# The last residual turned inside the first block of rows, its last weight sum moved to VectorE, and the restored chunks of y split one by one

## The chip, the cores and the metric

The kernel runs on one NeuronCore of a Trainium2 chip. The metric is the device time of one execution in microseconds, the lower the better. The engines are TensorE (PE, with its weight loads as PEld), VectorE (DVE), ScalarE (ACT), GpSimd (POOL) and SyncE (SP), which issues most transfers.

## The reference

One inference step of a hybrid decoder layer, for 512 prompt tokens and 8 x 4 sample tokens, width 2048: an input projection, an mLSTM branch, a sliding-window attention branch, a gated merge, an output projection, a residual and a layer norm. The change lies in the last lines of the merge:

```python
y = (jax.nn.sigmoid(g_m) * jnp.einsum('btc,cd->btd', br_m, w_proj_m)
     + jax.nn.sigmoid(g_a) * jnp.einsum('btc,cd->btd', br_a, w_proj_a))
out = jnp.einsum('btc,cd->btd', y, w_out)
return _layernorm(DN_ALPHA * x + out, ln_w, ln_b).astype(x.dtype)
```

## The kernel before

All 544 tokens are worked at once, in tiles of 128 output columns by 544 tokens. Products are made of three fp32r products: an operand is split into a high part (a cast on ScalarE, L221 for weights, L283 for all else) and a low part (a subtraction on VectorE, L222 and L284), and high by high, high by low and low by high are summed in PSUM.

The output projection has 16 tiles of columns (ct). Tiles 0 to 3 are plain products. Tiles 4 to 13 are done in five pairs by `paired`, which computes two tiles with seven half products (steps n = 0 to 6) in place of eight, on sums of quarters of the weights and of y. `prepare` makes the weight sum of a step two steps ahead: with `acc` set, the sums other than that of n = 2 which go into one of their own operands are done by a DMA that adds (L684, issued by POOL), the others by VectorE (L686). `half_product` is the TensorE work (L706 with high weights, L708 with low), `gather` takes the seven results together into the two tiles O1 and O2 (L716 to L735; L735, at n = 6, writes the last quarter of O1, which is the state's `c21` after the change). TensorE runs in the order of the program text (a manual schedule); the other engines are ordered by a scheduler, within what `behind` demands.

A finished tile is spawned as `residual_task`: a later `tick` turns it on TensorE, four transposes for the rows of tokens (L1795) and one for 32 odd tokens (L1801), each into a PSUM tile `sm` of a pool of four banks, and VectorE adds it to the rows z (L1797) and zs (L1802). The 32 odd tokens are copied aside first by ScalarE (L1791).

The last 256 columns, tiles 14 and 15, are done the other way round: `rows_of(t)` takes y as the stationary operand and gives 128 tokens by 256 columns, in 16 chunks k of three matmuls (L1885), into one `sm` bank. Its weights, w3, come as four pieces of 512 KB (two halves of k by two column tiles), loaded by `land_rows` (L211) and split by `split_rows` (L283, L284). `add_rows` adds the block to z (L1867), takes its statistics and moments; `finish` normalises and stores (L1848, L1852, L1854). There are four blocks t = 0 to 3; the sample rows come between.

One quarter of y (y21, the even chunks for the second half of the tokens) has lost its place to other forms by then. `land_y21` loads them again from DRAM in three loads (3, 3 and 2 chunks; before, L1950), into tiles of the pool `raw2`, and `restore_y21` splits them into new y21 tiles in four splits. Blocks 2 and 3 of the rows and `sum_others(1)` (L2022) use them. `beside_output` is a list of such side work by step number, one step for each half product of the five pairs. The tail itself reads

```python
tick()
rows_of(0, {13: rest})
add_rows(0)
finish(0)
```

where `rest` ticks once more, exhausts `restored` and calls `sum_others(1)`; that is, ahead of chunk 13, in the order of TensorE and VectorE.

Of the kernel before, what the change touches and what calls it, by code (L numbers as in the profile page):

```python
# [18 lines left out]
ALU = mybir.AluOpType  # L19
# [61 lines left out]
def _build(tc, nc, i, o, es):  # L81
# [11 lines left out]
    V, A, G, PE = nc.vector, nc.scalar, nc.gpsimd, nc.tensor  # L93
# [60 lines left out]
    state = {}  # L154

    def tick():
        for g in list(live):
            if next(g, StopIteration) is StopIteration:
                live.remove(g)
# [65 lines left out]
    @contextmanager  # L225
    def behind(*what):

        with ExitStack() as st:
            for w in what:
                st.enter_context(tc.issue_after(state[w].ins))  # L230
            yield
# [50 lines left out]
    def hilo(src, hi, lo):  # L282
        state["hi"] = A.copy(hi, src)  # L283
        state["lo"] = V.tensor_tensor(out=lo, in0=src, in1=r32(hi), op=ALU.subtract)  # L284
# [394 lines left out]
    def prepare(w, n):  # L679


        def add(out, a, b):
            if w.get("acc") and out == a and n != 2:
                G.dma_start(out=w[out][:], in_=w[b][:], accum_op=ALU.add)  # L684
            else:
                V.tensor_tensor(out=w[out][:], in0=w[a][:], in1=w[b][:], op=ALU.add)  # L686
        if n == 1:
            w["t1"] = raw2()
            add("t1", "b11", "b12")
        elif n == 2:  # L690
            add("b11", "t1", "b22")
        w["hl", n] = split(w[("b11", "t1", "b11", "b21", "b12", "b22", "b21")[n]])
        if n == (1 if w.get("acc") else 3):
            add("b12", "b12", "b22")
        elif n == (3 if w.get("acc") else 4):
            add("b21", "b21", "b11")
# [13 lines left out]
    def gather(w, n):  # L710

        A0, D0, B0 = (w["bank", b][:, :HT] if ("bank", b) in w else None for b in range(3))
        sc = w["scale"]
        if n == 0:
            w["p1"] = pe_.tile([128, HT], F32, tag="p1", name=nm("p1"))
            A.activation(w["p1"][:], A0, AF.Copy, scale=sc)  # L716
            return
        if n == 1:
            w["O1"], w["O2"] = ev(), ev()
        c11, c21 = (w["O1"][:, c:c + HT] for c in (0, HT))  # L720
        c12, c22 = (w["O2"][:, c:c + HT] for c in (0, HT))
        p1 = w["p1"][:]
        if n == 1:
            A.activation(c11, D0, AF.Copy, scale=sc)  # L724
            G.tensor_tensor(out=c22, in0=p1, in1=c11, op=ALU.subtract)  # L725
        elif n == 2:
            V.scalar_tensor_tensor(c12, B0, sc, p1, op0=ALU.mult, op1=ALU.subtract)  # L727
        elif n == 3:
            A.activation(c11, A0, AF.Copy, scale=sc)
        elif n == 4:  # L730
            V.scalar_tensor_tensor(c22, B0, -sc, c22, op0=ALU.mult, op1=ALU.add)  # L731
        elif n == 5:
            V.scalar_tensor_tensor(c12, D0, sc, c12, op0=ALU.mult, op1=ALU.add)
        else:
            V.scalar_tensor_tensor(c21, B0, sc, p1, op0=ALU.mult, op1=ALU.subtract)  # L735

    AHEAD = 400

    def paired(work, first=iter(()), early=False):

        steps = [(w, n) for w in work for n in range(7)]
        ready = 0
        load_a(work[0])
        with nullcontext() if early else behind("raw"):
            load_b(work[0])
        for at, (w, n) in enumerate(steps):

            if early and at == 0:
                next(first)
            while ready < min(at + 3, len(steps)):  # L750
                with tc.high_priority(offset=AHEAD), (behind("wh", "wl") if at == 0 else nullcontext()):
                    prepare(*steps[ready])
                ready += 1
            p = at // 7 + 1
            if n == 4 and "fetch" in w:
                w["fetch"]()
            if p < len(work):
                if n == 3:
                    load_a(work[p])
                elif n == 4:  # L760
                    load_b(work[p])
            half_product(w, n)
            with tc.high_priority(offset=AHEAD):
                gather(w, n)
            next(first, None)
            if n == 6:
                w["end"](w["O1"], w["O2"])
            tick()
# [537 lines left out]
    last = last_sum(s4)  # L1306
# [285 lines left out]
    def form_tile(p, s):  # L1592
        return p.tile([128, 4, 2, HT], F32R, tag="act", name=nm(s))
# [94 lines left out]
    with tc.manual_schedule(engines={PE.engine}):  # L1688
        y11, y21, yo = [], [], ([], [])
# [188 lines left out]
    def rows_of(t, meanwhile={}):  # L1878
        ps = rows[t] = sm()
        at = (0, 128, 272, 400)[t]  # L1880
        for k in range(KT):
            if k in meanwhile:
                meanwhile[k]()
            for n, (a, p) in enumerate(TERMS):
                PE.matmul(ps[:, 0:G3 * 128], (yh, yl)[a](k, at, 128), w_rows(k, p),  # L1885
                          start=(k == 0 and n == 0), stop=(k == KT - 1 and n == 2))
# [51 lines left out]
    def land_rows(half, g):  # L1938
        pieces.append((half, slice(g * 128, g * 128 + 128), load_half(wo, (16 - G3 + g) * 128, half)))
# [4 lines left out]
            hilo(raw[:], *(w[:, :, cs] for w in w3[half]))  # L1944

    landed = []

    def land_y21(j0, n):
        st = raw2()[:].rearrange("p a b -> p (a b)")[:, 0:n * HT].rearrange("p (j t) -> p j t", t=HT)
        nc.sync.dma_start(st, d_y[2 * j0:2 * (j0 + n):2, :, HT:T].rearrange("k p t -> p k t"))  # L1950
        landed.append((j0, n, st))

    def restore_y21():
        for j0, n, st in landed:
            for j in range(j0, j0 + n):
                if j in (j0, 4):
                    e = min(j0 + n, 4) if j < 4 else j0 + n
                    hilo(st[:, j - j0:e - j0], *(y21[j // 4][:, j % 4:j % 4 + e - j, p] for p in range(2)))
                    yield

    def beside_output():

        s4.extend(form_tile(act3, "s4") for _ in range(2))
        todo = {11: [lambda: load_rows(2)], 18: [lambda: load_rows(3)],
                27: [lambda: land_rows(0, 0)], 30: [open_rows], 31: [split_rows, lambda: land_rows(0, 1)],
                32: [lambda: land_rows(1, 0), lambda: land_rows(1, 1)],
                33: [split_rows, lambda: land_y21(0, 3)],
                34: [split_rows, split_rows, lambda: land_y21(3, 3), lambda: land_y21(6, 2)]}
        for at in range(35):
            for f in todo.get(at, ()):  # L1970
                f()
            yield
# [18 lines left out]
    def projected(p):  # L1991
        ct = 4 + 2 * p

        def end(o1, o2):
            spawn(residual_task(ct, o1, 1))
            spawn(residual_task(ct + 1, o2, 1))
        return dict(wv=wo, cA=ct * 128, cB=ct * 128 + 128, scale=1.0, acc=True, kts=(slice(0, 16, 2), slice(1, 16, 2)), end=end)

    with tc.manual_schedule(engines={PE.engine}):
        paired([projected(p) for p in range(5)], beside_output(), early=True)  # L2000
    y21[:] = [form_tile(actS, "y21") for _ in range(2)]

    def ln_rows(name):
        out = []
# [5 lines left out]

    with behind("raw"):
        lw, lb = ln_rows("ln_w"), ln_rows("ln_b")
    restored = restore_y21()
    ysum = ev(512)[:].rearrange("p (k t) -> p k t", k=KT)
    both_ = ysum.rearrange("p (g j o) (c t) -> p g j o c t", g=2, o=2, c=2)

# [12 lines left out]
    sum_others(0, 2, 3)  # L2029
    with tc.manual_schedule(engines={PE.engine, V.engine}):  # L2030

        def rest():
            tick()
            for _ in restored:
                pass
            sum_others(1)

        tick()
        rows_of(0, {13: rest})
        add_rows(0)  # L2040
        finish(0)
        rows_of(1)
        add_rows(1)
        esY.close()
        d2 = pool(esY, "d2", 1)
        lwq, lbq = (d2.tile([128, 512], F32, name=nm("lnq"))[:] for _ in range(2))
        cq = d2.tile([128, 128], F32, name="cq")
        nc.sync.dma_start(cq[:], i["consts"][:, C_Q:C_Q + 128])
        for q in range(4):
            r, cs = slice(q * 32, q * 32 + 32), slice(q * 512, q * 512 + 512)  # L2050
            nc.sync.dma_start(lwq[r], i["ln_w"][cs].partition_broadcast(32))
            nc.sync.dma_start(lbq[r], i["ln_b"][cs].partition_broadcast(32))
        finish(1)
        parts = sample_rows()
        rows_of(2, {3: lambda: add_sample_rows(parts), 12: lambda: moments(4)})
        finish(4)
        add_rows(2)
        finish(2)
        rows_of(3)
        add_rows(3)  # L2060
        finish(3, (0, 1024, 1664, 2048))
# [31 lines left out]
```

## Time and profile before

| | |
|---|---|
| median of 3 runs | 2477.39 us (2476.89 to 2478.4) |
| the profiled execution | 2476.01 us, of which the span of the profile is 2474.1 |
| PE busy | 2450.5 us, 99% of the span |
| DVE busy | 1832.1 us, 74% |
| ACT busy | 1236.5 us, 50% |
| POOL busy | 389.3 us, 16% |
| last product of the five pairs, first L1885, first L1867 | 2426.36, 2431.78, 2439.23 us from the span's start |

A row of the timeline has the start and the duration in us, the engine, the line, the operation, what is written and read, the count, and in brackets how long the engine had been idle and what ended that. Rows of stretches have the stretch, its length, then for PE, PEld, DVE, ACT and POOL the busy time and the number of instructions, then the granted clock of TensorE (1.00 is full), the busy share of the DMA engines, and GB/s. A row of waits says who waited for whom, for how long in total, how often, and the longest wait.

### The profile page before, as it was taken

What the parts mean: (1) busy time and instruction counts of PE and PEld (TensorE: products, weight loads), DVE (VectorE), ACT (ScalarE), POOL (GpSimd) and SP (SyncE); (2) the same over time, 40 slices, a digit from 0 to 9 for tenths busy, and PEclk for the clock granted to TensorE, in tenths of its full rate; (3) what the DMA queues carried; (4) which work ended last, traced back from release to release, by engine and by line L of the source; (5) the groups of instructions that cost most, each with busy time, mean ns of one, the idle gap of its engine ahead of it and who ended that gap; (6) DMA issues with size and microseconds to landing.
All of it is one profiled execution on the core that took longest, in us unless ns stands there. A gap on an engine that the chain in (4) does not pass through costs nothing. (4 is left out here: it accounts for less than half of the span.)

```text
span 2474.1 us, 48874 instructions
## 1 busy us (share of the span) xinstructions
PE 2450.5 (99%) x19631; PEld 2388.1 (97%) x19631; DVE 1832.1 (74%) x2697; ACT 1236.5 (50%) x2016; POOL 389.3 (16%) x458
## 2 busy tenths in 40 slices
PE   9999999999999999999999999999999999999997
PEld 9999999999999999999999999999999999999996
DVE  5687777777777777788778788887865557777767
ACT  4457766766766775443433444444633324434431
POOL 2121111111111111121111221200000002111211
PEclk9999999999999999999999999999999999999999
DMA  5675666666666545468577575786554549988875
GB/s 162 184 182 139 153 160 157 151 151 160 151 158 159 139 125 152 125 189 264 172 237 250 168 239 173 227 247 180 178 178 162 168 154 285 236 231 232 214 185 162
DMA packets 556803, 453.96 MB, mean 183 GB/s; under 512 B 42833, under 2 KB 465809, under 8 KB 556513
## 3 DMA queue, kind: packets, MB, share of 16 engines
q1 hardware_dynamic: 542448, 399.86, 54.8%
q0 software_dynamic: 14128, 50.99, 11.3%
q8 instruction: 154, 2.52, 0.4%
q14 instruction: 73, 0.59, 0.1%
HBM read 309.37 MB, written 94.22 MB: 163 GB/s over the span
## 5 line engine op out<-in xcount | busy, mean ns | idle before, releaser
L221 ACT CAST wh<-raw 128x1024 fp32r<-128x1024 f32 x640 | 670.3, 1048 | 811.6 <-PE bank L706 649.8
L222 DVE TENSOR_TENSOR wl<-raw,wh 128x1024 fp32r<-128x1024 f32 x640 | 794.8, 1244 | 260.5 <-ACT wh L221 259.2
L686 DVE TENSOR_TENSOR raw<-raw,raw 128x1024 f32<-128x1024 f32 x242 | 309.4, 1278 | 11.5 <-DMA raw<-in_w_in 3.8
L706 PE MATMUL bank<-xk,wh 128*128 128x272 f32 x2272 | 311.6, 289 | 0.0
L706 PEld LDWEIGHTS bank<-xk,wh 128*128 128x128 f32 x2272 | 293.6, 188 | 3.4 <-issue 2.5
L725 POOL TENSOR_TENSOR ev<-p,ev 128x272 f32<-128x272 f32 x84 | 124.7, 1484 | 577.0 <-ACT ev L724 546.9
L708 PE MATMUL bank<-xk,wl 128*128 128x272 f32 x1136 | 164.8, 287 | 0.0
L708 PEld LDWEIGHTS bank<-xk,wl 128*128 128x128 f32 x1136 | 151.4, 188 | 0.0
L684 POOL DMA_DIRECT2D raw<-raw x94 | 81.0, 862 | 446.2 <-DVE raw L686 228.8
L706 PE MATMUL bank<-s4h,wh 128*128 128x272 f32 x568 | 146.8, 291 | 0.0
L706 PE MATMUL bank<-s1h,wh 128*128 128x272 f32 x568 | 146.6, 291 | 0.1
L706 PE MATMUL bank<-n3h,wh 128*128 128x272 f32 x568 | 145.6, 289 | 0.5 <-DVE ev L727 0.5
L706 PE MATMUL bank<-a11h,wh 128*128 128x272 f32 x568 | 145.9, 289 | 0.0
L706 PE MATMUL bank<-n2h,wh 128*128 128x272 f32 x568 | 145.2, 289 | 0.0
L706 PE MATMUL bank<-a11l,wh 128*128 128x272 f32 x568 | 145.1, 288 | 0.0
L706 PE MATMUL bank<-n3l,wh 128*128 128x272 f32 x568 | 144.8, 288 | 0.0
L706 PE MATMUL bank<-s4l,wh 128*128 128x272 f32 x568 | 144.6, 287 | 0.0
L706 PE MATMUL bank<-s1l,wh 128*128 128x272 f32 x568 | 144.6, 287 | 0.0
L706 PE MATMUL bank<-n2l,wh 128*128 128x272 f32 x568 | 144.6, 287 | 0.0
L731 DVE SCALAR_TENSOR_TENSOR ev<-bank,ev 128x272 f32<-128x272 f32 x84 | 37.0, 441 | 125.7 <-PE bank L708 125.6
L246 PE MATMUL bank<-bh,wh 128*128 128x272 f32 x512 | 109.1, 292 | 0.0
L246 PE MATMUL bank<-bh,wl 128*128 128x272 f32 x512 | 108.9, 289 | 0.0
(563 smaller groups left out, 5851.1 us busy)
## 6 DMA issues: line engine op xcount, KB each, us to landing
raw<-in_w_in SPq DMA_DIRECT2D x296, 512.0 KB, 4.9
raw<-raw POOLq DMA_DIRECT2D x94, 512.0 KB, 4.9
C<-in_state_mlstm_C SPq DMA_DIRECT2D x32, 1024.0 KB, 6.5
out<-C SPq DMA_DIRECT2D x64, 512.0 KB, 3.5
raw<-in_w_proj_a SPq DMA_DIRECT2D x32, 512.0 KB, 4.8
raw<-in_w_proj_m SPq DMA_DIRECT2D x32, 512.0 KB, 6.1
raw<-in_w_out SPq DMA_DIRECT2D x32, 512.0 KB, 5.8
d_sga<-ev SPq DMA_DIRECT2D x16, 272.0 KB, 2.0
```

Of the source, the lines that this page charges most:

```text
L221: state["wh"] = A.copy(wh[:], raw[:])
L222: state["wl"] = V.tensor_tensor(out=wl[:], in0=raw[:], in1=r32(wh[:]), op=ALU.subtract)
L246: PE.matmul(ps[ALL, f, 0:w], a[:, kk], b(k, c, w), start=(k == 0 and n == 0), stop=(k == 15 and n == 2))
L684: G.dma_start(out=w[out][:], in_=w[b][:], accum_op=ALU.add)
L686: V.tensor_tensor(out=w[out][:], in0=w[a][:], in1=w[b][:], op=ALU.add)
L706: PE.matmul(ps, wh[:, k], x(p, k), start=(first and k == 0 and p == 0), stop=False, skip_group_check=True)
L708: PE.matmul(ps, wl[:, k], x(0, k), start=False, stop=(k == 7), skip_group_check=True)
L725: G.tensor_tensor(out=c22, in0=p1, in1=c11, op=ALU.subtract)
L731: V.scalar_tensor_tensor(c22, B0, -sc, c22, op0=ALU.mult, op1=ALU.add)
```

## The change

Three things. In `prepare`, the sum of n = 3 of the last pair (marked `last`) is made by VectorE in place of the adding DMA. The first load of y21 stands at step 30 of the side work, its tiles are made at step 33, and the first of the four splits is done there; a split of y21 is held behind `c21` of the pair before. In the tail, the restoring and `sum_others(1)` come ahead of chunk 1 of the first block, and the two ticks that turn the last pair's tiles come ahead of chunk 10, no tick ahead of the block.

```diff
         def add(out, a, b):
-            if w.get("acc") and out == a and n != 2:
+            if w.get("acc") and out == a and n != 2 and not (n == 3 and "last" in w):
                 G.dma_start(out=w[out][:], in_=w[b][:], accum_op=ALU.add)
...
-            V.scalar_tensor_tensor(c21, B0, sc, p1, op0=ALU.mult, op1=ALU.subtract)
+            state["c21"] = V.scalar_tensor_tensor(c21, B0, sc, p1, op0=ALU.mult, op1=ALU.subtract)
...
+    def open_y21():
+        y21[:] = [form_tile(actS, "y21") for _ in range(2)]
...
-                    hilo(st[:, j - j0:e - j0], *(y21[j // 4][:, j % 4:j % 4 + e - j, p] for p in range(2)))
+                    with behind("wh", "wl", "c21"):
+                        hilo(st[:, j - j0:e - j0], *(y21[j // 4][:, j % 4:j % 4 + e - j, p] for p in range(2)))
                     yield
+
+    restored = restore_y21()
...
-                27: [lambda: land_rows(0, 0)], 30: [open_rows], 31: [split_rows, lambda: land_rows(0, 1)],
+                27: [lambda: land_rows(0, 0)], 30: [open_rows, lambda: land_y21(0, 3)],
+                31: [split_rows, lambda: land_rows(0, 1)],
                 32: [lambda: land_rows(1, 0), lambda: land_rows(1, 1)],
-                33: [split_rows, lambda: land_y21(0, 3)],
+                33: [open_y21, split_rows, lambda: next(restored)],
                 34: [split_rows, split_rows, lambda: land_y21(3, 3), lambda: land_y21(6, 2)]}
...
-        paired([projected(p) for p in range(5)], beside_output(), early=True)
-    y21[:] = [form_tile(actS, "y21") for _ in range(2)]
+        paired([projected(p) for p in range(4)] + [projected(4) | {"last": True}], beside_output(), early=True)
...
-        def rest():
-            tick()
+        def restore():
             for _ in restored:
                 pass
             sum_others(1)

-        tick()
-        rows_of(0, {13: rest})
+        def residual():
+            tick()
+            tick()
+
+        rows_of(0, {1: restore, 10: residual})
```

How the order of the instructions changes. First TensorE, from the last product of the pairs on; ev_28807 and ev_28808 are O1 and O2, ox the 32 odd tokens. Before:

```order
-L708 MATMUL bank_28823<-yo_27037,wl_28887 128x272 x4
-L1795 MATMUL sm_28998<-cc,ev_28807 128x128 x4
-L1801 MATMUL sm_29004<-cc,ox_27130 32x128
-L1795 MATMUL sm_29008<-cc,ev_28808 128x128 x4
-L1801 MATMUL sm_29014<-cc,ox_27131 32x128
-L1885 MATMUL sm_29017<-w_3817_28811,y_3585_26880 128x256
```

and after, with the chunks between left out:

```order
+L708 MATMUL bank_28825<-yo_27037,wl_28889 128x272 x4
+L1885 MATMUL sm_28999<-w_3817_28811,y_3585_26880 128x256
...
+L1885 MATMUL sm_28999<-w_3819_28813,yo_27038 128x256
+L1795 MATMUL sm_29039<-cc,ev_28807 128x128 x4
+L1801 MATMUL sm_29045<-cc,ox_27130 32x128
+L1795 MATMUL sm_29049<-cc,ev_28808 128x128 x4
+L1801 MATMUL sm_29055<-cc,ox_27131 32x128
+L1885 MATMUL sm_28999<-w_3819_28813,y_3603_27036 128x256
```

The ten transposes moved behind the tenth chunk; the block's sum sm_28999 now takes its bank ahead of the four turned tiles, and the last of these, sm_29055, takes the bank of the first, sm_29039.

Then VectorE at the same place, from the last quarter of O1 to the first L1867. Before:

```order
-L735 SCALAR_TENSOR_TENSOR ev_28807<-bank_28823,p_3807_28755 128x272
-L1797 SCALAR_TENSOR_TENSOR z_27816<-z_27816,sm_28998 128x4x128
-L1802 SCALAR_TENSOR_TENSOR zs<-zs,sm_29004 32x128
-L1797 SCALAR_TENSOR_TENSOR z_27816<-z_27816,sm_29008 128x4x128
-L1802 SCALAR_TENSOR_TENSOR zs<-zs,sm_29014 32x128
-L284 TENSOR_TENSOR y_3834_28978<-raw_3831_28917,y_3834_28978 128x3x272
-L284 TENSOR_TENSOR y_3834_28978<-raw_3832_28948,y_3834_28978 128x272
-L284 TENSOR_TENSOR y_3835_28979<-raw_3832_28948,y_3835_28979 128x2x272
```

and after:

```order
+L735 SCALAR_TENSOR_TENSOR ev_28807<-bank_28825,p_3807_28755 128x272
+L284 TENSOR_TENSOR y_3832_28917<-raw_3834_28952,y_3832_28917 128x272
+L284 TENSOR_TENSOR y_3833_28918<-raw_3834_28952,y_3833_28918 128x2x272
+L284 TENSOR_TENSOR y_3833_28918<-raw_3835_28954,y_3833_28918 128x2x272
+L2026 TENSOR_TENSOR ev_28990<-y_3832_28917 128x4x16
+L2026 TENSOR_TENSOR ev_28990<-y_3833_28918 128x4x16
+L1797 SCALAR_TENSOR_TENSOR z_27816<-z_27816,sm_29039 128x4x128
+L1802 SCALAR_TENSOR_TENSOR zs<-zs,sm_29045 32x128
```

Three splits of y21 and the two sums (L2022 before, L2026 after) moved ahead of the residual's additions; the first and largest split moved further up, ahead of the splits of the last two pieces of weights.

Last, VectorE at the sum of n = 3 of the last pair (raw_28600 is the weight quarter that is added to raw_3797_28635). After:

```order
+L2030 TENSOR_TENSOR ev_28990<-yo_27037,yo_27038 128x4x16 x2
+L686 TENSOR_TENSOR raw_3797_28635<-raw_3797_28635,raw_28600 128x1024
+L727 SCALAR_TENSOR_TENSOR ev_28808<-bank_28825,p_3807_28755 128x272
+L222 TENSOR_TENSOR wl_28822<-raw_28602,wh_28821 128x1024
 L284 TENSOR_TENSOR w_3818_28812<-raw_28691,w_3817_28811 128x8x128
```

L686 was not there before, and L684 of the same tiles has gone from POOL's queue, where it stood last ahead of the five L1831. SP's loads keep their order, of weights and of y. The second, third and fourth piece of weights are loaded into the three tiles `raw`; before, the second took the place of the one read by the low split of n = 4, the third that of the source of the adding DMA, the fourth that of the first piece. After, the second takes the place of L686's source, the third that of the tile split for n = 4, the fourth again that of the first piece.

More of the change, by code (lines that the diff above doesn't have):

```diff
@@ L2012, in _build @@
         lw, lb = ln_rows("ln_w"), ln_rows("ln_b")
-    restored = restore_y21()
     ysum = ev(512)[:].rearrange("p (k t) -> p k t", k=KT)
```

## The prediction

> **What bounds the kernel now.** I read the page's busy shares, then the chain that ended last, then VectorE's waits behind the chain's first row, and then went backwards through the timeline.
>
> ```profile
> PE 2450.5 (99%) x19631; PEld 2388.1 (97%) x19631; DVE 1832.1 (74%) x2697; ACT 1236.5 (50%) x2016; POOL 389.3 (16%) x458
> ```
> ```profile
> 2442.06 0.49 DVE z L1848
> ...
> 2469.06 0.53 DVEq L2089
> ```
> ```profile
> DVE z L1867 <- PE sm L1885: 3.2, 1, 3.2
> DVE mv L1828 <- PE sm L1827: 0.5, 1, 0.5
> DVE zs L1837 <- POOL mv L1831: 0.4, 1, 0.4
> ```
>
> Over the span TensorE is the bound (99%), but the chain from 2442 on is VectorE's. Behind the first L1867 (the first block of rows is added to the residual) VectorE waits only twice more, 0.5 and 0.4 us, both inside the normalisation of the sample rows, which the change leaves alone. So the end lies a fixed time behind that first L1867, and what moves it moves the end by as much. What stands ahead of it, in the timeline and then in stretches of 2 us (the clock is the third number from the right):
>
> ```profile
> 2427.37 0.38 PE L1795 MATMUL sm<-cc,ev 128*128 128x128 f32 x2
> 2427.85 1.04 ACT L283 CAST w<-raw 128x1024 fp32r<-128x1024 f32 x1 [1.02 <-DMA raw<-in_w_out]
> 2428.93 1.23 DVE L284 TENSOR_TENSOR w<-raw,w 128x1024 fp32r<-128x1024 f32 x1 [1.26 <-ACT w L283]
> 2429.01 1.51 ACT L283 CAST y<-raw 128x272 fp32r<-128x272 f32 x3
> 2430.07 0.43 DVE L735 SCALAR_TENSOR_TENSOR ev<-bank,p 128x272 f32<-128x272 f32 x1
> ...
> 2430.56 0.44 PE L1795 MATMUL sm<-cc,ev 128*128 128x128 f32 x2 [2.81 <-DVE ev L735]
> ...
> 2431.04 0.69 DVE L1797 SCALAR_TENSOR_TENSOR z<-z,sm 128x512 f32<-128x512 f32 x1 [0.53 <-PE sm L1795]
> ...
> 2431.78 1.01 PE L1885 MATMUL sm<-w,y 128*128 128x256 f32 x3
> ...
> 2433.10 2.63 DVE L284 TENSOR_TENSOR y<-raw,y 128x816 fp32r<-128x816 f32 x4
> ...
> 2435.65 0.35 DVE L2022 TENSOR_TENSOR ev<-y 128x64 f32<-128x64 f32 x2
> ...
> 2438.68 0.52 PE L1885 MATMUL sm<-w,yo 128*128 128x256 f32 x3
> ...
> 2439.03 0.51 PE L1885 MATMUL sm<-w,y 128*128 128x256 f32 x3
> ...
> 2439.23 0.42 DVE L1867 SCALAR_TENSOR_TENSOR z<-z,sm 128x256 f32<-128x256 f32 x1 [3.23 <-PE sm L1885]
> ```
> ```profile
> 2444.32 0.52 PE L1885 MATMUL sm<-w,yo 128*128 128x256 f32 x3
> ```
> ```profile
> 2430.00:2432.00 2.00, 1.35 (x9) 0.97 (x10) 1.44 (x4) 0.81 (x3) 0.00 (x0) 0.93 1.04 416
> 2432.00:2434.00 2.00, 2.00 (x10) 2.00 (x11) 1.91 (x4) 0.00 (x0) 0.00 (x0) 0.50 0.49 197
> 2434.00:2436.00 2.00, 2.00 (x15) 2.00 (x14) 2.00 (x6) 0.00 (x0) 0.00 (x0) 0.72 0.13 37
> ```
>
> TensorE comes to the turning of the last pair's first tile at 2427.37, does two transposes, and stands 2.81 us: the tile's last quarter (L735) is queued on VectorE behind the split of the last piece of weights (L284 at 2428.93), which waits for ScalarE's cast (2427.85), which waits for that piece's load. Then the granted clock falls to 0.50. The 16 chunks of the first block take 2431.78 to 2439.03, 7.25 us; at full clock a chunk takes (2444.32 - 2439.03) / 15 = 0.353 us and 16 of them 5.65. From 2427.37 to L1867 it is 11.86 us.
>
> **The change part by part.**
>
> *Rows before the residual.* After: TensorE starts the block's chunks where the transposes stood, at 2427.37. Ten chunks end at 2430.90. What the turning costs there, from the pair before, where nothing waited:
>
> ```profile
> 2408.24 0.60 PE L1795 MATMUL sm<-cc,ev 128*128 128x128 f32 x4
> ...
> 2408.68 0.27 PE L1801 MATMUL sm<-cc,ox 128*32 128x128 f32 x1
> ...
> 2408.79 0.60 PE L1795 MATMUL sm<-cc,ev 128*128 128x128 f32 x4
> ...
> 2409.22 0.27 PE L1801 MATMUL sm<-cc,ox 128*32 128x128 f32 x1
> ```
>
> The second L1801 follows 0.98 us behind the first L1795, at 2431.88. Here it must wait: the block's sum holds one of the four PSUM banks, so this fifth tile takes the bank of the first turned tile and needs VectorE's L1797 to have read it. Four transposes (0.60) end at 2431.50; L1797 starts 0.04 later, as after the transposes of 2430.56, takes 0.69, and TensorE follows 0.05 later, as at 2431.78: 2432.28, a wait of 0.40 that before did not exist. The next chunk is 0.11 behind it (2408.68 to 2408.79), the sixteenth five chunks on (2432.39 + 1.77 = 2434.16), and L1867 0.55 behind the start of the sixteenth (2438.68 to 2439.23): 2434.71 instead of 2439.23, 4.52 us earlier. Of this 2.81 is the idle time, 1.60 the slow clock (7.25 - 5.65), the rest the order. The bounds here: with no wait at the fifth tile 4.9; and a group after a short wait can last 0.1 longer, 4.4.
>
> The term of 1.60 rests on the clock's following the gap. The trace has it once: 4.4 us without a product (2427.37 to 2431.78, with the transposes and the stand), then 0.50 for about 3 us, then 1.00. The Trainium skill ("TensorE: Matmul & The Clock Gate", Part 1) says that the clock is halved after an idle window of about 3.4 us and comes back after a busy one, that the window runs freely, so that the place of the change varies from run to run, and (Part 4) that transposes do not count as busy. By that rule an execution whose window lay otherwise would show no slow chunks before the change, and the sum would be 2.9 instead of 4.5; the trace agrees with the rule, as far as one fall in one execution can. The turning behind chunk 10, 1.5 us without a product, is shorter than the stand that preceded this fall.
>
> *The last sum on VectorE.* One L686 is added there, one L684 leaves POOL's queue.
>
> ```profile
> 2404.03 1.23 DVE L686 TENSOR_TENSOR raw<-raw,raw 128x1024 f32<-128x1024 f32 x1
> ...
> 2415.65 0.89 POOL L684 DMA_DIRECT2D raw<-raw  x1 [1.85 <-DVE wl L222]
> ...
> 2416.08 0.43 DVE L727 SCALAR_TENSOR_TENSOR ev<-bank,p 128x272 f32<-128x272 f32 x1
> ...
> 2418.35 2.16 PE L706 MATMUL bank<-n,wh 128*128 128x272 f32 x16
> ...
> 2420.79 1.05 ACT L221 CAST wh<-raw 128x1024 fp32r<-128x1024 f32 x1 [1.78 <-DMA raw<-raw]
> ...
> 2421.63 0.44 DVE L731 SCALAR_TENSOR_TENSOR ev<-bank,ev 128x272 f32<-128x272 f32 x1 [1.72 <-PE bank L708]
> ```
>
> L686 stands ahead of L727, so L727 and three splits move by 1.23 us. TensorE's L706 at 2418.35 adds onto the bank that L727 reads; L727 now ends at 2416.08 + 1.23 + 0.43 = 2417.74, 0.6 in time. The splits are made up for by L731, ahead of which VectorE idled 1.72. Price nothing; if that cover were gone, 1.23 less the 0.6, that is 0.6 us, on TensorE. POOL has nothing else to do there, so its 0.89 brings nothing; the sum's transfer had held up the cast at 2420.79, and no product waited for that.
>
> *Loads.* SP's order keeps its places; what each load waits for changes.
>
> ```profile
> 2417.67 4.04 SPq L211 DMA_DIRECT2D raw<-in_w_out  x3
> ...
> 2421.80 2.01 SPq L1950 DMA_DIRECT2D raw<-d_y  x2
> ...
> 2422.81 1.05 ACT L283 CAST w<-raw 128x1024 fp32r<-128x1024 f32 x1 [0.97 <-DMA raw<-in_w_out]
> ```
> ```profile
> SPq L211 <- DMA raw<-raw: 3.1, 2, 2.6
> ```
>
> Before, the second of three weight loads waited 2.6 us for the transfer of the sum to let go of its source; that is gone. Now they are free at L686's end (2417.3), at the end of the moved split (2416.43 row's place + 1.2: about 2418.9) and one split later (about 2420), so the last is issued near 2420 instead of 2421.3. Landing took 5.1 us (2417.67 to 2422.81) and for the last one 6.5 (to 2427.85): it lands between 2425.1 and 2426.5. Cast and split (1.04, 1.23) end by 2428.9, and L735, whose product ends at 2427.5, by 2429.3. Chunk 8, the first that needs these weights, comes at 2427.37 + 8 x 0.353 = 2430.19; the tile's last quarter is wanted at 2431.1. Both are hidden behind the chunks, with 1.3 and 1.8 us to spare.
>
> *Restored chunks.* Their first split moves ahead; the other three (1.64 of the 2.63, by elements) and the two L2022 (0.35) now stand between L735 and L1797: 2429.3 + 2.0 = 2431.3, 0.2 ahead of the 2431.54 at which L1797 wants to start. This is the narrowest cover; each us beyond it costs one. The last load of y is issued behind the split of the pair's last weights as before (by 2423.8, the end of that row), and in the trace of before its cast was never late (three casts from 2429.01 without a gap, so it had landed by 2430.0).
>
> Sum: 4.5 us off the profiled execution's 2476.01, 2471.5. That execution lies 1.4 under the median of the runs, 2477.39; taken off the median, 2472.9.
>
> **The rivals.** *The loads land no sooner.* The 1.04 and 1.23 of the last piece then stay at 2427.85 and 2428.93, L735 ends at 2430.5, the three splits and L2022 at 2432.5, and L1797 starts 0.9 late; chunk 8 still finds its weights (2430.16 against 2430.19). Gain 3.6, 2473.8. For it: the last piece took 6.5 us among the loads of y and the norm's weights, which stay. Against: its issue moves by 1.3 us and 512 KB of traffic go.
>
> *The slow clock isn't the gap's.* If runs without the profiler never fell to 0.50 there, or fall after the change too, 1.60 of the 4.5 is lost: gain 2.9, 2474.5. For it: 2.81 us is short, and the row of 2430 shows 0.93 still, so that the fall came about 1.3 us after TensorE had started again. Against: the clock is 1.00 in all neighbouring stretches. The page's freely running window, weighed above, would be its cause.
>
> *Slower.* VectorE takes its queue in order, so the last load of y now stands ahead of L1797, and so of TensorE's fifth tile, and of all that follows. From its landing to L1797 it is 0.5 (cast), 0.7 (split), 0.35. It costs nothing until 2430.0, then one for one; beyond 2.8 us the clock would fall again. The gain is gone when it lands at about 2433, some 9.5 us after its issue. The longest median in the list of transfers around here is 7.7, for the norm's weights, queued behind it:
>
> ```profile
> ln<-in_ln_w SPq DMA_DIRECT2D x2, 512.0 KB, 7.7
> ```
>
> **How the numbers follow.** Forecast (gain 3.9 to 4.9) 0.62; loads no sooner (3.2 to 3.9) 0.16; clock (2.4 to 3.2) 0.13; slower 0.04; something unseen 0.05. The likeliest gives 2472.9. The range runs from a gain of 5.5 (no wait at the fifth tile, and half a us of spread: the runs before span 1.5) to one of 2.4: 2471.9 to 2475.0. The line of 0.2%, about what a measurement of this kernel can tell from no change, is 4.95 us: just beyond the forecast. Of the forecast's share, spread carries some 0.25 over it; the rest of it and the two smaller gains stay within: 0.68; slower by 0.2% needs the last rival at its worst or something unseen, 0.06; faster with the unseen 0.26.
>
> **What would show it.** Right: no idle time before the first L1885, chunks of 0.353 us and a clock of 1.00 from 2424 to 2436, L1795 after ten chunks, a wait near 0.4 at the second L1801, L1867 near 2434.7, and behind it the same 35 us to the end. Wrong: a PE wait before chunk 8 or at L1795 (weights or L735 late), L1797 waiting on a split of y, an L706 at 2418 waiting for L727, or a first L1867 as early as forecast with VectorE waiting more often behind it.

## The result and the profile after

| | before | after |
|---|---|---|
| median of 19 runs each, us | 2476.3 (2473.82 to 2478.4) | 2471.94 (2469.96 to 2475.11) |
| the profiled execution: time, span, us | 2476.01, 2474.1 | 2471.94, 2469.8 |
| start of the pairs' last L708 | 2426.36 | 2426.62 |
| first L1867 | 2439.23 | 2434.98 |
| from the one to the other, "the stretch" | 12.87 | 8.36 |
| from first L1867 to the end of the span | 34.87 | 34.82 |

The ratio of the times is 0.9984, with a 95% interval of 0.9977 to 0.999, a gain of 2.5 to 5.7 us. The forecast was 2472.9, a gain of 4.5, within 2471.9 to 2475.0.

The page's busy shares, and then VectorE's waits from 2430 us on (who waited for whom, total, times, longest):

```profile
PE 2448.2 (99%) x19631; PEld 2386.4 (97%) x19631; DVE 1830.9 (74%) x2698; ACT 1236.5 (50%) x2016; POOL 384.3 (16%) x457
```
```profile
DVE z L1797 <- PE sm L1795: 1.3, 1, 1.3
DVE z L1867 <- PE sm L1885: 1.1, 1, 1.1
DVE mv L1828 <- PE sm L1827: 0.5, 1, 0.5
DVE zs L1837 <- POOL mv L1831: 0.4, 1, 0.4
```

TensorE is as full as before and one L686 has come to VectorE (2697 to 2698). Behind the first L1867 stand the same two waits, 0.5 and 0.4, and the same 35 us. The whole gain is ahead of that instruction, and there the timeline shows it:

```profile
2425.93 1.05 ACT L283 CAST w<-raw 128x1024 fp32r<-128x1024 f32 x1 [1.01 <-DMA raw<-in_w_out]
2426.62 1.17 PE L708 MATMUL bank<-yo,wl 128*128 128x272 f32 x8
2427.55 1.52 ACT L283 CAST y<-raw 128x272 fp32r<-128x272 f32 x3 [0.57 <-DMA raw<-d_y]
2427.63 0.52 PE L1885 MATMUL sm<-w,y 128*128 128x256 f32 x3
...
2428.16 0.43 DVE L735 SCALAR_TENSOR_TENSOR ev<-bank,p 128x272 f32<-128x272 f32 x1
...
2428.51 1.70 DVE L284 TENSOR_TENSOR y<-raw,y 128x272 fp32r<-128x272 f32 x3
...
2430.13 0.35 DVE L2026 TENSOR_TENSOR ev<-y 128x64 f32<-128x64 f32 x2
...
2431.16 0.60 PE L1795 MATMUL sm<-cc,ev 128*128 128x128 f32 x4
...
2431.80 0.69 DVE L1797 SCALAR_TENSOR_TENSOR z<-z,sm 128x512 f32<-128x512 f32 x1 [1.32 <-PE sm L1795]
...
2432.54 0.28 PE L1801 MATMUL sm<-cc,ox 128*32 128x128 f32 x1 [0.23 <-DVE z L1797]
...
2434.98 0.42 DVE L1867 SCALAR_TENSOR_TENSOR z<-z,sm 128x256 f32<-128x256 f32 x1 [1.15 <-PE sm L1885]
```

The chunks begin right behind the last product, without the stand of 2.81 us. L735 is done 2.6 us before the transposes at 2431.16 want its tile. VectorE is idle 1.32 ahead of L1797, which waits for TensorE and for nothing else. The one new wait is the forecast one, at the second L1801. In the stretches of 2 us (the clock is third from the right) TensorE is full but for that wait, at 1.00:

```profile
2430.00:2432.00 2.00, 2.00 (x20) 1.99 (x19) 0.68 (x4) 0.00 (x0) 0.00 (x0) 1.00 0.99 396
2432.00:2434.00 2.00, 1.77 (x16) 1.53 (x15) 1.74 (x4) 0.00 (x0) 0.00 (x0) 1.00 0.96 206
2434.00:2436.00 2.00, 2.00 (x20) 2.00 (x19) 0.98 (x2) 0.00 (x0) 0.00 (x0) 1.00 0.31 74
```

### The profile page after: what moved, and what is told of

Its sections match the earlier page's. It is cut to its first block, busy times and chain, and to the rows that moved or that the text cites. A ratio compares the mean times of both kernels' runs of the same rounds, so it can differ in the third digit from the quotient of the medians.

```text
span 2469.8 us, 48872 instructions
## 1 busy us (share of the span) xinstructions
PE 2448.2 (99%) x19631; PEld 2386.4 (97%) x19631; DVE 1830.9 (74%) x2698; ACT 1236.5 (50%) x2016; POOL 384.3 (16%) x457
## 3 DMA queue, kind: packets, MB, share of 16 engines
q8 instruction: 154, 2.52, 0.4%
## 5 line engine op out<-in xcount | busy, mean ns | idle before, releaser
L686 DVE TENSOR_TENSOR raw<-raw,raw 128x1024 f32<-128x1024 f32 x243 | 308.8, 1271 | 11.4 <-DMA raw<-in_w_in 3.2
L708 PE MATMUL bank<-xk,wl 128*128 128x272 f32 x1136 | 164.7, 287 | 0.0
L708 PEld LDWEIGHTS bank<-xk,wl 128*128 128x128 f32 x1136 | 151.4, 188 | 0.0
L684 POOL DMA_DIRECT2D raw<-raw x93 | 80.3, 863 | 445.7 <-DVE raw L686 213.5
L731 DVE SCALAR_TENSOR_TENSOR ev<-bank,ev 128x272 f32<-128x272 f32 x84 | 37.0, 441 | 125.2 <-PE bank L708 125.1
```

Source lines behind the costliest of these rows:

```text
L708: PE.matmul(ps, wl[:, k], x(0, k), start=False, stop=(k == 7), skip_group_check=True)
```

## The experiments

The start of the last L708 lay between 2424.37 and 2428.67 us in the executions below. An edit in the tail does not explain that, so single executions are compared by the stretch, not by their total.

| kernel | last L708 | first L1867 | stretch | time, us |
|---|---|---|---|---|
| sum on VectorE alone | 2427.46 | 2436.68 | 9.22 | 2472.64, median of 11 |
| residual at chunk 10 alone | 2428.67 | 2438.74 | 10.07 | 2475.4 |
| changed kernel, sum by DMA | 2426.64 | 2435.37 | 8.73 | 2472.31 |
| changed kernel, y split late | 2428.01 | 2436.37 | 8.36 | 2473.02 |
| before + 24 products | 2425.65 | 2436.78 | 11.13 | 2473.45 |
| before + 26 transposes | 2425.89 | 2437.67 | 11.78 | 2474.48 |
| before, second execution | 2424.57 | 2435.73 | 11.16 | 2472.47 |
| before, third execution | 2427.05 | 2439.57 | 12.52 | 2476.26 |
| changed kernel, residual at chunk 4 | 2424.37 | 2433.73 | 9.36 | 2470.6 |
| changed kernel, own bank | 2426.94 | 2434.89 | 7.95 | 2471.86 |
| the same, timed | 2426.97 | 2434.92 | 7.95 | 2471.27, median of 11 |

**The sum on VectorE alone**, in the kernel before:

```diff
-            if w.get("acc") and out == a and n != 2:
+            if w.get("acc") and out == a and n != 2 and not (n == 3 and "last" in w):
...
-        paired([projected(p) for p in range(5)], beside_output(), early=True)
+        paired([projected(p) for p in range(4)] + [projected(4) | {"last": True}], beside_output(), early=True)
```

> The kernel before with one edit: the last sum made by VectorE. The residual stays ahead of the rows. Theory (the late loads made the gap, the gap made the clock fall): L735 ends near 2428.6 instead of 2430.5, TensorE idles 0.9 us instead of 2.81, the clock stays at 1.00, the first L1885 starts near 2429.9: stretch 9.3 to 9.4, gain 3.5 of the 4.5. Rival A (the clock falls with the shorter gap too): 10.9 to 11.0, gain 1.9. Rival B (the sum does not bring the loads forward): 12.9, no gain.

SP's waits between 2405 and 2425 us, of the kernel before and then of this one:

```profile
SPq L211 <- DVE wl L222: 9.7, 1, 9.7
...
SPq L211 <- DMA raw<-raw: 3.1, 2, 2.6
```
```profile
SPq L211 <- DVE raw L686: 9.9, 1, 9.9
...
SPq L211 <- DVE wl L222: 1.0, 1, 1.0
SPq L211 <- DVE w L284: 0.7, 1, 0.7
```

And its timeline:

```profile
2426.63 1.05 ACT L283 CAST w<-raw 128x1024 fp32r<-128x1024 f32 x1 [0.96 <-DMA raw<-in_w_out]
...
2428.85 0.43 DVE L735 SCALAR_TENSOR_TENSOR ev<-bank,p 128x272 f32<-128x272 f32 x1
...
2429.34 0.44 PE L1795 MATMUL sm<-cc,ev 128*128 128x128 f32 x2 [0.72 <-DVE ev L735]
...
2430.16 0.28 PE L1801 MATMUL sm<-cc,ox 128*32 128x128 f32 x1 [0.38 <-ACT ox L1791]
```

The wait of SP for the adding transfer is gone. The long waits of 9.7 and 9.9 us are those of the first of the three loads for a free tile, and both kernels have one. The last piece is cast 0.83 ahead of the last L708 where it was 1.49 behind it, 2.3 us sooner, and TensorE's stand shrinks from 2.81 to 0.72, with 0.38 more for the copy of the odd tokens. Of the 2.3 us, 1.5 are the earlier issue: the last L211 starts 6.7 us ahead of the last L708 (at 2420.8) where it started 5.2 ahead (2421.2). The other 0.8 is a quicker landing. The edit also takes the 512 KB of the adding transfer away, and whether that is the reason is not shown.

All thirteen executions agree: in the seven with the adding transfer L735 starts 3.3 to 3.8 us behind the start of the last L708, in the six with the sum on VectorE 1.4 to 2.1.

The stretch is 9.22: this line alone brings 3.65 of the 4.51 us in that pair of executions. The median of 2472.64 against 2475.94 beside it has the ratio 0.9988, interval 0.9979 to 0.9997.

**The residual at chunk 10 alone**, in the kernel before:

```diff
...
-        tick()
-        rows_of(0, {13: rest})
+        rows_of(0, {10: residual, 13: restore})
```

Here `residual` ticks twice, and `restore` does what `rest` did without its tick.

> Only the residual's place is changed: it is turned ahead of chunk 10, y21 is restored ahead of chunk 13 as before, and the last sum stays an adding DMA. The measure is the stretch from the start of the last product of the pairs (L708) to the first L1867: 12.87 us before (2426.36 to 2439.23), 8.36 after (2426.62 to 2434.98). Theory (order on VectorE and late loads both count): no idle time of TensorE and full clock, but L735 ends near 2430.5, the additions of the residual follow at 2431.5, and only behind them the four splits of y21 and the two L2022 (2.63 + 0.35 us), so that VectorE comes to L1867 at about 2436.6: stretch 10.2, gain 2.6. Rival (the residual's place does it alone): stretch 8.4, gain 4.5.

```profile
2432.28 0.43 DVE L735 SCALAR_TENSOR_TENSOR ev<-bank,p 128x272 f32<-128x272 f32 x1
...
2435.91 2.63 DVE L284 TENSOR_TENSOR y<-raw,y 128x816 fp32r<-128x816 f32 x4
2438.46 0.35 DVE L2022 TENSOR_TENSOR ev<-y 128x64 f32<-128x64 f32 x2
2438.74 0.41 DVE L1867 SCALAR_TENSOR_TENSOR z<-z,sm 128x256 f32<-128x256 f32 x1
```

TensorE stands nowhere but for 0.24 us at the second L1801, the clock is 1.00, and L1867 no longer waits for TensorE (no bracket): VectorE comes to it late, from the restored chunks. The stretch is 10.07. So what holds L1867 has changed from TensorE to VectorE, and the place of the restoring matters once the residual is late. The parts do not add up: 3.65 and 2.80 alone, 4.51 together. Most of that is the slow clock, which the first execution of before has and which either part alone avoids: against a second execution of before whose clock did not fall (11.16, below) they are 1.94 and 1.09 alone and 2.80 together.

**The changed kernel with the sum by the adding DMA:**

```diff
-            if w.get("acc") and out == a and n != 2 and not (n == 3 and "last" in w):
+            if w.get("acc") and out == a and n != 2:
```

> The changed kernel with the last sum made by the adding DMA again. Theory (the sum on VectorE is what brought the weight loads forward): the last piece's cast is back near 2427.9 instead of 2425.9, L735 ends near 2430.5 instead of 2428.6, the three splits of y21 and the two sums push L1797 to about 2432.4, 0.6 to 0.9 later than 2431.8: stretch 9.0 to 9.3 instead of 8.36. Rival (the loads came sooner because of the loads of y, or their cover is wide enough): 8.4.

```profile
2429.95 0.43 DVE L735 SCALAR_TENSOR_TENSOR ev<-bank,p 128x272 f32<-128x272 f32 x1
2430.31 1.70 DVE L284 TENSOR_TENSOR y<-raw,y 128x272 fp32r<-128x272 f32 x3
...
2431.93 0.35 DVE L2026 TENSOR_TENSOR ev<-y 128x64 f32<-128x64 f32 x2
2432.20 0.68 DVE L1797 SCALAR_TENSOR_TENSOR z<-z,sm 128x512 f32<-128x512 f32 x1
...
2432.93 0.28 PE L1801 MATMUL sm<-cc,ox 128*32 128x128 f32 x1 [0.60 <-DVE z L1797]
```

Here the prediction's rival "the loads land no sooner" is made on purpose. Its mechanism appears: L1797 has no idle time ahead of it, and TensorE waits 0.60 in place of 0.23 for it. It costs 0.37 (8.73 against 8.36), where the prediction had priced 0.9 and the expectation 0.6 to 0.9: against the last L708, L735 ends 0.4 earlier than the rival put it, and the splits and sums behind it take 1.8 us, not 2.0. Beside the other two parts, the VectorE sum is worth far less than alone, where it brought 3.65 against the first execution of before and 1.94 against the second.

**The changed kernel with the restored chunks split late** (loaded and split where before had it, still ahead of chunk 1 in program order):

```diff
-                27: [lambda: land_rows(0, 0)], 30: [open_rows, lambda: land_y21(0, 3)],
+                27: [lambda: land_rows(0, 0)], 30: [open_rows],
...
-                33: [open_y21, split_rows, lambda: next(restored)],
+                33: [split_rows, lambda: land_y21(0, 3)],
...
+    open_y21()
```

> The changed kernel with the first load of y21 at step 33 again and its tiles made behind the pairs, so that all four splits of y21 stand between L735 and L1797. In the trace after, L735 ends at 2428.5. Theory (VectorE has room now): 2428.5 + 2.63 + 0.35 = 2431.5, ahead of the 2431.8 at which L1797 starts: stretch 8.4, the early split brings nothing. Rival (the cover was as narrow as forecast, 0.2 us): the first split's 1.0 us shows, stretch 9.1 to 9.4.

```profile
2429.76 2.62 DVE L284 TENSOR_TENSOR y<-raw,y 128x816 fp32r<-128x816 f32 x4
...
2433.19 0.69 DVE L1797 SCALAR_TENSOR_TENSOR z<-z,sm 128x512 f32<-128x512 f32 x1 [0.55 <-PE sm L1795]
```

Four splits instead of three stand ahead of L1797, and it still waits 0.55 for TensorE. The stretch is the changed kernel's, 8.36: the early load and split of the first three chunks bring nothing that this place shows.

**Filling the stand**, for the clock's term. In the kernel before, ahead of the first `tick()`, 24 products (or, in the second kernel, 26 transposes of the other tile) into a bank that nobody reads:

```diff
+        dummy = bank()
+        for _ in range(24):
+            PE.matmul(dummy[:, 0:G3 * 128], yh(0, 0, 128), w_rows(0, 0), start=True, stop=True)
         tick()
         rows_of(0, {13: rest})
```

> The kernel before with 24 extra products (128x256, y by w3, into a spare bank, their sum used by nobody) between the last product of the pairs and the transposes of the residual; at 0.118 us each they take 2.8 us, the time that TensorE stood. Theory (the clock falls because of the stand): the clock stays at 1.00, 16 chunks take 5.65 us instead of 7.25, the stretch from the last L708 to the first L1867 is 11.2 to 11.3 instead of 12.87. Rival (the fall has another cause, such as the load on VectorE or DMA at that time): the clock falls to 0.50 all the same, 12.9.

> The kernel before with 26 extra transposes (128x128, of a finished tile, into a spare bank, used by nobody) at the same place; at 0.11 us each also 2.8 us. The Trainium skill (TensorE: Matmul & The Clock Gate, Part 4) says that transposes do not count as busy; by that the clock falls as before and the stretch is 12.9. Rival (any work of TensorE holds the clock): 1.00, stretch 11.2 to 11.4.

```profile
2426.65 2.97 PE L2040 MATMUL bank<-w,y 128*128 128x256 f32 x24
```
```profile
2427.44 3.06 PE L2041 MATMUL bank<-cc,ev 128*128 128x128 f32 x26 [0.39 <-DVE ev L733]
```

The clock stayed at 1.00 with both; the stretches are 11.13 and 11.78. The 26 transposes began 0.39 late and ended behind L735, hence the 0.65 more. Taken alone, that would make the stand the cause of the fall. Two more executions of the kernel before, unchanged, put it in doubt.

> The kernel before once more, unchanged, for the term of 1.60 us. My theory: the slow clock follows TensorE's stand, so the granted clock falls to about 0.50 behind the first product of the first block again, and from the start of the pairs' last L708 to the first L1867 it is 12.9 us. Rival (a window that runs freely decides, and it can lie otherwise): the stand of 2.8 us is there, the clock stays at 1.00, and the stretch is 11.3 us. With only a part of the slow time inside the block it lies between.

> A third execution of the kernel before, for the same question as the second. Theory: clock 0.50 for about 3 us behind the stand, 12.9 us from the start of the last L708 to the first L1867. Rival: clock 1.00, 11.3 us.

The second execution, first the timeline, then one of its stretches; then three of the third execution's:

```profile
2428.55 0.44 PE L1795 MATMUL sm<-cc,ev 128*128 128x128 f32 x2 [2.58 <-DVE ev L735]
...
2435.73 0.42 DVE L1867 SCALAR_TENSOR_TENSOR z<-z,sm 128x256 f32<-128x256 f32 x1 [1.74 <-PE sm L1885]
```
```profile
2430.00:2432.00 2.00, 2.00 (x19) 2.00 (x18) 1.91 (x4) 0.00 (x0) 0.00 (x0) 1.00 0.57 227
```
```profile
2430.00:2432.00 2.00, 0.66 (x3) 0.59 (x4) 1.28 (x2) 1.59 (x5) 0.00 (x0) 0.77 1.03 412
2432.00:2434.00 2.00, 2.00 (x12) 1.94 (x11) 1.80 (x4) 0.00 (x0) 0.00 (x0) 0.50 1.01 406
2434.00:2436.00 2.00, 2.00 (x17) 2.00 (x17) 1.97 (x4) 0.00 (x0) 0.00 (x0) 0.88 0.08 31
```

The second stands nearly as long as the first (2.58 us, the first 2.81) and the clock does not fall: 11.16, close to the rival's 11.3. In the third, which stands 2.90, it falls, a little earlier against the stand than in the first, so that part of the slow time lies inside the wait: 12.52. Worked out from the clock column, the slow time is 3.4 us in both (0.93, 0.50 and 0.72 in the three stretches that the prediction shows of the first, 0.77, 0.50 and 0.88 here). So both fillings, one execution each, do not settle it: without them one execution of three shows 1.00 as well. That filling the gap prevents the fall is not shown.

**The residual at chunk 4**, in the changed kernel:

```diff
-        rows_of(0, {1: restore, 10: residual})
+        rows_of(0, {1: restore, 4: residual})
```

> The changed kernel with the residual turned ahead of chunk 4 instead of 10. Theory (VectorE's order: L1797 stands behind the splits of y21 and the two sums, which end at 2430.5 in the trace after): the transposes start at 2429.04, the second L1801 would come at 2430.0 but waits for L1797, which ends near 2431.2: a wait of 1.2 us in place of 0.4, stretch 9.1 to 9.2. Rival (the place among the chunks does not matter): 8.4.

```profile
2426.78 0.61 PE L1795 MATMUL sm<-cc,ev 128*128 128x128 f32 x4
...
2428.15 0.35 DVE L2026 TENSOR_TENSOR ev<-y 128x64 f32<-128x64 f32 x2
2428.43 0.68 DVE L1797 SCALAR_TENSOR_TENSOR z<-z,sm 128x512 f32<-128x512 f32 x1
...
2429.16 0.28 PE L1801 MATMUL sm<-cc,ox 128*32 128x128 f32 x1 [1.23 <-DVE z L1797]
```

The transposes are ready for VectorE while it still splits y; L1797 comes behind L2026 without a gap, and TensorE waits 1.23. The stretch of 9.36 is 1.0 longer than with chunk 10, a little more than the 9.1 to 9.2 expected. Its time of 2470.6 is low only because this execution reached the last L708 2.25 us before the changed kernel's.

**A bank of its own for the first block's sum**, so that the fifth turned tile need not wait, in one execution and then in eleven:

```diff
-        ps = rows[t] = sm()
+        ps = rows[t] = bank() if t == 0 else sm()
```

> The changed kernel with the sum of the first block of rows in a free bank of the pairs' pool, so that the last turned tile no longer waits for VectorE to read the first. Theory (the wait at the second L1801 is that shared bank): no wait there, the next L1885 0.4 us earlier, stretch 7.9 to 8.0 instead of 8.36. Rival (the wait is VectorE's, so the time comes back at L1867): 8.3 to 8.4.

> The changed kernel with the first block's sum in the pool of the seven half products in place of a bank of sm, now timed. My theory: the wait of 0.4 us at the second L1801 is gone again and nothing else moves, so the stretch from the last L708 to the first L1867 is 7.9 to 8.0 us, and the time is 0.4 us below the changed kernel's: 2471.5, a ratio to the kernel before of 0.9980 to 0.9983. Rival: the gain of 0.4 is lost again behind the first L1867 (a second block that wants its bank back), ratio 0.9984 or more.

The timeline of the second, called "timed" in the table:

```profile
2431.51 0.60 PE L1795 MATMUL sm<-cc,ev 128*128 128x128 f32 x4
...
2432.49 0.27 PE L1801 MATMUL sm<-cc,ox 128*32 128x128 f32 x1
...
2434.92 0.42 DVE L1867 SCALAR_TENSOR_TENSOR z<-z,bank 128x256 f32<-128x256 f32 x1 [0.74 <-PE bank L1885]
```

The second L1801 follows the first L1795 by 0.98 without a wait; both executions give 7.95, 0.41 less than the changed kernel, and behind L1867 the span ends 34.8 us later as before, so the rival's loss there does not come. The median of 2471.27 has the ratio 0.9979 (0.997 to 0.9988) to the kernel before. It is the best version here, but its interval overlaps with the changed kernel's: the 0.41 is shown by the stretch, not by the time.

## Why the prediction was right, point by point

- *Rows before the residual.* Behind the last product everything fell where it was put, 0.26 later as this execution's last L708 was: L1797 at 2431.80 (2431.54 forecast), the second L1801 at 2432.54 (2432.28), L1867 at 2434.98 (2434.71). The new wait costs 0.40 as worked out: the second L1801 starts 1.38 behind the first L1795, 0.98 without a wait (its bracket has 0.23, the part in which the profile shows TensorE idle). The own bank takes away 0.41.
- *The stand of 2.81.* Right: it is gone, and the sum on VectorE alone brings it to 0.72. So most of it came from the last piece's load, which the adding transfer held up, through SP's wait for its source by 1.5 us, and perhaps through its traffic.
- *The clock's 1.60.* The weak step, and its size holds only for the execution that was shown. The first L1885 to L1867 takes 7.45 us in the first execution of before, 5.97 in the second: 1.48 for a full fall. Against the changed kernel's 8.36, the three executions of before give gains of 4.51, 2.80 and 4.16, a mean of 3.8. The prediction says that single executions can differ, but it priced this, at 0.13 and 2.9 us, as a fact that holds for all runs or for none. The clock fell in two of these three, and three cannot say how often it does. The prediction also read the fall as following 4.4 us without a product, transposes left out; the last section has rows that speak against leaving them out. What was forecast is what the first execution does; the medians differ by 4.36, and their interval does not separate 3.8 from 4.5. That the gain came so close to 4.5 is in part luck.
- *The last sum on VectorE.* Price nothing, right. The idle time ahead of L731 was 1.72 and is now 0.58, in the changed kernel's timeline:

```profile
2421.89 0.44 DVE L731 SCALAR_TENSOR_TENSOR ev<-bank,ev 128x272 f32<-128x272 f32 x1 [0.58 <-PE bank L708]
```

  So it took 1.14 of the 1.23 us, and the cover held with 0.58 to spare.
- *Loads.* The last piece was forecast to land between 2425.1 and 2426.5 and was cast at 2425.93.
- *Restored chunks.* "The narrowest cover", 0.2 us, was in fact 1.3 (L1797 idle 1.32). L735 was taken from the late bound of the landing, to end by 2429.3; it ended at 2428.59. With all four splits behind L735, 0.55 was left. The slower rival, a late last load of y, did not come: its cast, the last of the three from 2427.55, started at 2428.4, so it had landed at least 1.6 us before the 2430.0 from which it would have cost time.
- *The number.* The 2472.9 was taken off a median of three runs, 2477.39. Over nineteen runs the median of before is 2476.3, and the same gain taken off that is 2471.8. So the gain was forecast better than the time, which lies at the very edge of the range.

## What to carry to other kernels

Where a transfer that adds in place reads a buffer that a queued load wants, the price is not in the add but in the load: here moving one such sum to VectorE took away SP's wait of 2.6 us for it and 2.1 of the 2.8 us that TensorE stood, several queues further on. When work is put between a producer and a late consumer, look for what runs out instead, a bank of PSUM (0.40 us here) or the next engine's queue (1.0 us more with the same work six chunks sooner). A fall of the clock behind a short gap should be priced by its frequency over a few profiled executions, not by the one at hand.

## What was not expected of the hardware

The length of TensorE's stand alone did not decide whether the granted clock fell. In the tail it still could have: waits of 2.81 and 2.90 us were followed by a fall, one of 2.58 and one of 0.72 were not. But the clock also falls in some executions at the kernel's start, which no edit touches, where TensorE waits for the first tokens. In the timeline, the kernel with its own bank (timed) and then the one with the residual alone:

```profile
4.86 1.06 PE L350 MATMUL sm<-cc,xin 128*128 128x128 f32 x4
...
10.30 1.53 PE L350 MATMUL sm<-cc,xin 128*128 128x128 f32 x12 [2.30 <-DMA xin<-in_x_prompt]
...
15.25 0.60 PE L350 MATMUL sm<-cc,xin 128*128 128x128 f32 x4
```
```profile
10.59 2.52 PE L350 MATMUL sm<-cc,xin 128*128 128x128 f32 x12 [2.06 <-DMA xin<-in_x_prompt]
```

The wait of 2.30 leaves the same twelve transposes at 1.53 us, the wait of 2.06 slows them to 2.52, and the stretch behind it has

```profile
12.00:14.00 2.00, 2.00 (x14) 1.63 (x12) 1.69 (x5) 1.38 (x5) 0.00 (x0) 0.50 1.17 321
```

Of the other executions, the one with y split late fell behind a wait of 2.09, and the changed kernel with the sum by DMA kept its clock behind 2.40. The third execution of before fell in its opening too, but only at about 14.4 us (its stretch from 14 to 16 us has 0.61), long after its wait of 1.16, behind which the twelve still took 1.53. The Trainium skill ("TensorE: Matmul & The Clock Gate", Part 1) has a window that runs freely and is not reset when a kernel starts. These rows agree, in that a wait of nearly the same length ends either way; they do not show the window itself.

The opening also bears on what the 26 transposes left open. Until the twelve at 10.30, TensorE has run nothing but transposes (L344, which turns the identity, and L350), and it has come from slow to fast on them: four take 1.06 us at 4.86, as four L1795 do at a clock of 0.50 in the third execution of before (at 2432.04), and four take 0.60 at 15.25. The twelve take 1.53 us, which is fast beside the 2.52 at the slow clock. The clock column reads 1.00 in these first stretches, so the durations decide here. So transposes did raise the clock, against the rule drawn on above that they do not count as busy.

The opening is also one source of the differing starts of the last L708, but not the only one: the second execution of before came to it 1.8 us sooner than the first, with no fall of the clock in either opening. Where those 1.8 us lie stays open.
